# A two-layer hybrid decoder trunk on one core: statistics sent in 128-byte pieces, a held ScalarE half of a split, and 512-column projections

## The chip, the core and the metric

The kernel runs on one core of a Trainium2 chip. The core has a matrix engine (TensorE, PE in the profile; its weight loads are listed apart as PEld), a vector engine (VectorE, DVE), a scalar engine (ScalarE, ACT), GpSimd (POOL), and SyncE (SP), which here only issues transfers. Sixteen DMA engines move data between the large off-chip memory (HBM) and the on-chip memory (SBUF); matmuls write to PSUM, which has eight banks of 128 x 512 float32. Each engine takes its own instructions strictly in the order in which they stand in its queue, so one instruction that waits holds up all behind it.

The metric is device time in microseconds (us) of one execution. Lower is better.

## What is computed

256 tokens of width 1024 pass through two layers. Each layer does

```
h = layer_norm(a*x + 0.5*swiglu(x, ffn1))          # swiglu: (silu(x@Wg) * (x@Wu)) @ Wdown, Wdown 2816 x 1024
o = [deltanet(h), window_attention(h), memory_attention(h, mem_n)]
h = layer_norm(a*h + (sum_n sigmoid(gate_n) * (o_n @ w_branch_n)) @ w_out)
h = layer_norm(a*h + 0.5*swiglu(h, ffn2))
```

with a = (2*2)**0.25. `mem_n` is a layer norm of 256 memory rows, computed once: `(mem - mean) * rsqrt(var + 1e-5) * g + b`. All weights are float32 and each is used once, so the kernel reads some 220 MB of weights.

## The kernel before

**Three products for one.** Each weight tile arrives in float32 (`raw`, 128 x 1024, 512 KB) and is split in two: ScalarE rounds it to a shorter format (`whi`, line 116) and VectorE takes the remainder (`wlo`, line 117). Activations are split in the same way (`hT`, `u0` to `u10`, `w0` to `w3`). `mm3` then makes three matmuls: high x high, high x low, low x high. One raw tile with its two halves is a *unit*. There are three `raw` buffers and five each of `whi` and `wlo`; `unit` asks for a load on SyncE's queue and gives it a priority 300 places ahead of the program, so loads and splits run ahead of the matmuls as far as buffers allow.

**A feed-forward block (`Ffn`)** has eleven steps of 256 hidden columns. In a step four units make two banks (tokens 0 to 127 and 128 to 255; gate columns in the left half, up columns in the right). `out(i, banks)` then applies silu on ScalarE (line 339) and the product on VectorE (line 340), transposes 32 x 32 blocks on VectorE (line 343), and turns the rest through HBM: four small stores (`tr<-t`, line 349) and a load (`pt<-tr`, line 350), all on GpSimd's queue. `settle` splits the landed `pt` into the high and low halves of `u_i` (ScalarE's is the 128 x 512 cast `u<-pt`, VectorE's follows). The settlement of step i stands in `out(i+2)`, and those of the last two steps in the down projection. `issue_after(x)` adds, for the instructions inside it, an order behind `x` on the engine of `x` only. `settle` gives it a VectorE instruction in `out` and a matmul in the down projection, so ScalarE's cast was free to stand anywhere in ScalarE's queue that the scheduler chose.

**The down projection (`projA`)** takes 22 units of 128 x 1024 (the output projection of the mixers takes 8). The first two units (`lead`) are run for one half of the tokens and then for the other; the following ones for both in turn; the last 4 or 6 (`tail`) bank by bank, so that each bank is finished while the next is still computed. `full_rows` gives the banks: tokens 0 to 127 have two of 512 columns, tokens 128 to 255 have one of 512 (`c`), one of 256 (the left half of `d`) and one of 256 in another pool (`at`). The short last banks keep the work after the last matmul small. `Post` adds each finished bank to the residual (`src`, line 394) and does the layer norm.

**The memory statistics** are made beside the first layer's first feed-forward block: `mid` hangs pieces on certain steps. `rows_` computes mean and 1/std for 256 rows into `mst` (one number a partition, four columns), stores them to HBM transposed (line 454) and loads them back to all partitions as `gB` (line 456). `half(0)` and `half(1)` subtract, scale and split (lines 466 to 471), and `keep` stores the result (`mdr`, line 431, four transfers of 512 KB) for the second layer. Lines 454, 456, 349 and 350 share GpSimd's queue.

**Places in SBUF.** The pool `pu` hands out places in the order in which its tags are first asked for, each rounded up to 32 bytes of a partition: `hT`, `u0`, `u1`, `u2`, then `mst` (16 bytes, takes 32), `mgb` (64), `w0` to `w3`, `u3` and the rest. The pools `p2` and `p3` follow.

Of the kernel before, what the change touches and what calls it, by code (L numbers as in the profile page):

```python
# [17 lines left out]
P = 128  # L18
# [20 lines left out]
def tile_trunk(ctx, tc, x, xT, mem, memT_, wst, lnp, memln, cvw, rows, cst, out):  # L39
# [54 lines left out]
        nc.scalar.copy(t.rearrange("p v k -> p (v k)"), zero.to_broadcast([P, 2 * S]))  # L94


    pos = [0]

    def unit(w=U, dst=None, cuts=1, behind=None):
        ahead = tc.high_priority(offset=AHEAD) if pos[0] >= 8 * P * U else nullcontext()  # L100
        raw = T(praw, [P, U], "raw")
        src = wst[pos[0]:pos[0] + P * w].rearrange("(p w) -> p w", p=P)
        pos[0] += P * w
        (ph, th), (pl, tl) = dst or ((phi, "whi"), (plo, "wlo"))
        with ahead:
            hi = T(ph, [P, U], th, F32R)
            lo = T(pl, [P, U], tl, F32R)
            for i in range(cuts):
                c = slice(i * w // cuts, (i + 1) * w // cuts)
                nc.sync.dma_start(raw[:, c], src[:, c])  # L110
                with tc.issue_after(behind) if behind else nullcontext():
                    split(hi[:, c], lo[:, c], raw[:, c])
        return hi, lo

    def split(hi, lo, src):
        nc.scalar.copy(hi, src)  # L116
        return nc.vector.tensor_tensor(lo, src, hi.bitcast(F32), op=ALU.subtract).ins  # L117

    pinned = [False]

# [10 lines left out]
    def mm3(o, l, r, first, last, skip=False):  # L131
        (lh, ll), (rh, rl) = l, r
        matmul(o, lh, rh, start=first, stop=False, skip_group_check=skip)
        matmul(o, lh, rl, start=False, stop=False, skip_group_check=skip)
        return matmul(o, ll, rh, start=False, stop=last, skip_group_check=skip).ins

    def weave(work, steps):

# [31 lines left out]
            (b,) = yield from projB_parts(xt, 2, 4)  # L170
            use(i, b)

    def projA(xt, w, kpu, nk, outs, tail=0, dsts=(), lead=0, after=None, behind=None, held=(), led=None, along=None):

        def one(k, kk, hi, lo, tb, j):
            ts = slice(tb * P, (tb + 1) * P)
            n = [o.shape[-1] for o in outs[tb]]
            c = kk * w + sum(n[:j])
            c = slice(c, c + n[j])
            return mm3(outs[tb][j], (xt[0](k)[:, ts], xt[1](k)[:, ts]), (hi[:, c], lo[:, c]), k == 0, k == nk - 1)  # L180

        nu = nk // kpu
        units = {}

        def get(uu):
            if uu not in units:
                t = uu - (nu - tail)
                units[uu] = unit(kpu * w, dsts[t] if 0 <= t < len(dsts) else None, behind=behind if uu in held else None)
            return units[uu]

        def run(us, tb, js):
            ins = None
            for uu in us:
                for kk in range(kpu):
                    for j in js:
                        ins = one(uu * kpu + kk, kk, *get(uu), tb, j)
            return ins

        for tb in range(2):
            if lead:  # L200
                run(range(lead), tb, range(len(outs[tb])))
            if led:
                led(tb)
        for uu in range(lead, nu - tail):
            for tb in range(2):
                ins = run([uu], tb, range(len(outs[tb])))
# [88 lines left out]
    class Ffn:  # L295
# [37 lines left out]
        def out(self, i, banks):  # L333


            t = T(p2, [P, 8, 2, 32], "t2", bufs=4)
            for tb in range(2):
                g, u = (banks[tb][:, c:c + S].rearrange("p (j x) -> p j x", j=8) for c in (0, S))
                nc.scalar.activation(t[:, :, tb, :], g, AF.Silu)  # L339
                ins = nc.vector.tensor_tensor(t[:, :, tb, :], t[:, :, tb, :], u, op=ALU.mult).ins  # L340
            self.last = ins
            z = T(p2, [P, 512], "t2", bufs=4)
            ins = nc.vector.transpose(z, t.rearrange("p j t x -> p (j t x)")).ins  # L343
            if len(self.due) > 1:
                self.settle(ins)
            y = T(p2, [P, D], "pt")[:, 0:512]
            d = T(pd, [4, 32, 4, P], "tr")
            for q in range(4):
                nc.gpsimd.dma_start(d[:, :, q].rearrange("b c x -> c b x"), z[32 * q:32 * q + 32].rearrange("c (b x) -> c b x", b=4))  # L349
            nc.gpsimd.dma_start(y, d.rearrange("b c q x -> (b c) (q x)"))  # L350
            self.due.append((i, y))

        def settle(self, behind):

            if self.due:
                i, y = self.due.pop(0)
                hi, lo = (self.h(i)[:, n].rearrange("p a (t q s) -> p (a t) q s", t=2, q=4) for n in range(2))
                with tc.issue_after(behind):
                    split(hi, lo, y.rearrange("p (q n s) -> p n q s", q=4, n=4))

        def rest(self, hT, tail, dsts, post, mid={}, behind=None):
            for i in range(1, NFT // 2):
                banks = [acc() for _ in range(2)]
                for uu in range(KD // 2):
                    hi, lo = unit(behind=behind if i == 1 and uu < 2 else None)
                    for kk in range(2):
                        k, c = 2 * uu + kk, slice(kk * 512, kk * 512 + 512)
                        for tb in range(2):
                            ts = slice(tb * P, (tb + 1) * P)
                            mm3(banks[tb], (hT[0][:, k, ts], hT[1][:, k, ts]), (hi[:, c], lo[:, c]), k == 0, k == KD - 1)  # L370
                self.out(i, banks)
                for f in (2 * i, 2 * i + 1):
                    if f in mid:
                        with tc.issue_after(self.last):
                            mid[f]()
            outs = full_rows()
            projA((lambda k: self.hu[k // 2][:, 0, k % 2, :], lambda k: self.hu[k // 2][:, 1, k % 2, :]), D, 1, NFT, outs, tail, dsts, 2, post, along=self.settle)
# [41 lines left out]
    def memory_T(mT, l):  # L419
# [11 lines left out]
                nc.gpsimd.dma_start(mdr[i], flat(t.bitcast(F32)))  # L431

        def vecs():
            got["st"] = T(pu, [P, 2, 2], "mst")
            got["gb"] = T(pu, [P, 2, KD], "mgb")
            load(got["gb"], memln)
            mT.extend(T(pu, [P, 4, S], f"w{i}", F32R) for i in range(4))
            got["m"] = [T(p2, [P, D], "pp") for _ in range(2)]
            for tb in range(2):
                load(got["m"][tb], mem[tb * P:(tb + 1) * P, :])  # L440

        def rows_():
# [11 lines left out]
            nc.gpsimd.dma_start(d.rearrange("a t p -> p a t"), got["st"])  # L454
            got["row"] = T(pu, [P, D], "gB")[:, 0:512]
            nc.gpsimd.dma_start(got["row"], d.rearrange("a t p -> (a t p)").partition_broadcast(P))

        def halves_():
            got["m"] = [T(p2, [P, 4, S], "pp") for _ in range(2)]
# [27 lines left out]
    def mixers(l, hT, mkT, mv_, post):  # L487
# [519 lines left out]
        def between(tb):  # L1007
            if tb == 0:
# [1 line left out]
                    merge_turn(1, q)  # L1010
                pinned[0] = False

        outs = full_rows()
        projA((lambda k: mgT[k // 4][:, k % 4, :], lambda k: mgT[2 + k // 4][:, k % 4, :]), D, 1, KD, outs, 6,
              [((pu, a), (pu, b)) for a, b in (("u6", "u7"), ("u10", "u11"), ("u12", "u13"), ("u0", "u1"), ("u2", "u3"), ("u8", "u9"))], 2, post, led=between)


    hT = new_hT()
# [129 lines left out]
```

## Time and profile before

| | |
|---|---|
| median of three timed runs | 1311.1 us (1308.61 to 1311.26) |
| the profiled execution's own time | 1317.82 us |
| its span, first to last instruction | 1315.8 us |
| mean granted TensorE clock | 0.99 |
| busy: PE, DVE, ACT, POOL | 1279.6, 849.7, 658.9, 197.8 us |
| HBM read, written | 247.45 MB, 14.81 MB |

The profile is one execution. Its own time is 2.0 us more than its span, and 6.7 us more than the median of the timed runs. PE's busy time counts overlapping matmuls, so it is nearly the whole span even though a single stretch may contain waits; these are found in the rows for stretches and in the timeline.

In rows of a stretch (the view of windows) stand: the stretch in us from the span's start, its length, then busy time and number of instructions of PE, PEld, DVE, ACT and POOL, the granted TensorE clock (1.00 is full), the mean busy share of the DMA engines, and GB/s. In rows of the timeline: start, duration, engine, line, operation, tiles, count, and in brackets the idle time before it with what ended it. In rows of the chain: start, duration, what. In rows of the waits: who waited for whom, us in total, times, longest. In rows on DMA issues: the transfer, the queue, the count, KB each, median us from issue to landing.

### The profile page before, as it was taken

Reading aid. Unit: us, or ns where it says so; the run is one execution under the profiler, and the core shown is the slowest. Engines: PE = TensorE matmul, PEld = TensorE weight load, DVE = VectorE, ACT = ScalarE, POOL = GpSimd, SP = SyncE. Lnnn points to the kernel's source line nnn. Section 1 sums busy time; section 2 is a strip of 40 time slices with the busy share of each in tenths; the row PEclk is TensorE's granted clock in tenths of the full one; section 3 lists DMA queues with packets and bytes.
Section 4 is the critical chain, followed back from the end, with each engine's and each line's share of the span. In section 5 each row is a group of like instructions: output and inputs, shape, how many; then the busy total and the mean of one; then the engine's idle time right before and its main releaser. Section 6 shows DMA issues by size and latency. Waiting matters only on the chain.

```text
span 1315.8 us, 19159 instructions
## 1 busy us (share of the span) xinstructions
PE 1279.6 (97%) x7160; PEld 1091.7 (83%) x7160; DVE 849.7 (65%) x1266; ACT 658.9 (50%) x979; POOL 197.8 (15%) x357
## 2 busy tenths in 40 slices
PE   8997799999999999999999999999999999999997
PEld 6885688999878788888878888899988787888786
DVE  5575547598564875665576665658966378666655
ACT  5544444565674444553444544446566654444441
POOL 0221200101411002221012220001023100022100
PEclk9998899999999999999999999999999999999999
DMA  7887765664643557786767786656554356477662
GB/s 258 297 266 182 241 221 169 193 189 147 160 145 114 181 170 226 240 254 214 251 205 252 241 259 212 207 162 208 167 145 156 97 175 225 145 253 250 224 207 105
DMA packets 77980, 263.52 MB, mean 200 GB/s; under 512 B 11872, under 2 KB 13024, under 8 KB 77888
## 3 DMA queue, kind: packets, MB, share of 16 engines
q1 hardware_dynamic: 66320, 232.53, 55.4%
q0 software_dynamic: 11568, 29.77, 7.6%
q8 instruction: 56, 0.92, 0.3%
q14 instruction: 36, 0.29, 0.1%
HBM read 247.45 MB, written 14.81 MB: 199 GB/s over the span
## 4 chain that ended last, share of the span: by engine, by line
PE 73%; DMA 13%; DVE 5%; ACT 5%; issue 3%; POOL 1%; SPq 0%; DVEq 0%; ACTq 0%; POOLq 0%
PE acc L126 62%; DMA raw<-in_wst_dram 8%; PE at L126 4%; DMA pt<-tr 3%; ACT whi L116 3%; PE sm L126 3%; DVE wlo L117 2%; DMA tr<-t 2%; PE sm L129 1%; DMA ms<-mst 1%; PE acc L321 1%; PE acc L318 1%; PE acc L319 1%; PE at L129 0%; POOL tr L349 0%
## 5 line engine op out<-in xcount | busy, mean ns | idle before, releaser
L117 DVE TENSOR_TENSOR wlo<-raw,whi 128x1024 fp32r<-128x1024 f32 (+2 forms) x403 | 483.3, 1212 | 352.4 <-ACT whi L116 350.9
L116 ACT CAST whi<-raw 128x1024 fp32r<-128x1024 f32 (+2 forms) x403 | 412.1, 1035 | 391.7 <-DMA raw<-in_wst_dram 222.2
L126 PE MATMUL acc<-whi,hT 128*128 128x512 f32 (+1 forms) x1824 | 567.7, 389 | 10.6 <-ACT whi L116 10.6
L126 PEld LDWEIGHTS acc<-whi,hT 128*128 128x128 f32 x1824 | 343.2, 190 | 80.4 <-ACT whi L116 11.8
L126 PE MATMUL acc<-wlo,hT 128*128 128x512 f32 (+1 forms) x912 | 353.3, 387 | 2.0 <-DVE wlo L117 1.9
L126 PE MATMUL acc<-whi,u 128*128 128x512 f32 (+1 forms) x800 | 253.0, 380 | 9.2 <-DVE t L340 9.2
L126 PEld LDWEIGHTS acc<-wlo,hT 128*128 128x128 f32 x912 | 172.9, 190 | 36.9 <-DVE wlo L117 4.3
L126 PEld LDWEIGHTS acc<-whi,u 128*128 128x128 f32 x800 | 152.4, 191 | 40.2 <-DVE t L340 9.3
L349 POOL DMA_DIRECT2D tr<-t x176 | 96.2, 553 | 387.9 <-DVE t L343 374.8
L126 PE MATMUL acc<-wlo,u 128*128 128x512 f32 (+1 forms) x400 | 150.6, 376 | 0.4 <-DVE wlo L117 0.4
L126 PE MATMUL acc<-hT,whi 128*128 128x256 f32 x672 | 122.2, 284 | 0.0
L126 PEld LDWEIGHTS acc<-hT,whi 128*128 128x128 f32 x672 | 104.7, 192 | 0.0
L126 PE MATMUL acc<-hT,wlo 128*128 128x256 f32 x336 | 95.1, 283 | 0.0
L126 PEld LDWEIGHTS acc<-wlo,u 128*128 128x128 f32 x400 | 76.8, 192 | 14.7 <-DVE wlo L117 0.8
L116 ACT CAST u<-pt 128x512 fp32r<-128x512 f32 x44 | 27.3, 620 | 105.5 <-DMA pt<-tr 105.5
L126 PEld LDWEIGHTS acc<-hT,wlo 128*128 128x128 f32 x336 | 64.4, 192 | 0.0
L350 POOL DMA_DIRECT2D pt<-tr x44 | 24.6, 558 | 156.3 <-DMA tr<-t 83.4
L117 DVE TENSOR_TENSOR u<-pt,u 128x512 fp32r<-128x512 f32 x44 | 29.0, 660 | 22.7 <-ACT u L116 22.7
L126 PE MATMUL at<-whi,u 128*128 128x256 f32 x152 | 39.7, 287 | 0.0
L340 DVE TENSOR_TENSOR t<-t,acc 128x256 f32<-128x256 f32 x88 | 36.3, 416 | 4.6 <-ACT t L339 3.5
L339 ACT ACTIVATE t<-acc 128x256 f32<-128x256 f32 x88 | 32.6, 376 | 10.6 <-PE acc L126 10.3
L516 DVE SCALAR_TENSOR_TENSOR t<-acc,cw,t 128x255 f32<-128x255 f32 (+2 forms) x72 | 34.5, 479 | 0.9
(249 smaller groups left out, 1263.5 us busy)
## 6 DMA issues: line engine op xcount, KB each, us to landing
raw<-in_wst_dram SPq DMA_DIRECT2D x409, 512.0 KB, 4.4
tr<-t POOLq DMA_DIRECT2D x176, 64.0 KB, 3.2
pt<-tr POOLq DMA_DIRECT2D x44, 256.0 KB, 4.9
raw<-in_wst_dram SPq DMA_DIRECT2D x16, 324.0 KB, 3.1
gB<-in_lnp_dram SPq DMA_DIRECT2D x6, 512.0 KB, 6.5
bB<-in_lnp_dram SPq DMA_DIRECT2D x6, 512.0 KB, 5.9
mdr<-w POOLq DMA_DIRECT2D x4, 512.0 KB, 7.2
w<-dr POOLq DMA_DIRECT2D x4, 512.0 KB, 12.2
```

The source lines that it names most:

```text
L116: nc.scalar.copy(hi, src)
L117: return nc.vector.tensor_tensor(lo, src, hi.bitcast(F32), op=ALU.subtract).ins
L126: return pe(nc.tensor.matmul(*a, **k))
L129: return pe(nc.tensor.transpose(*a))
L318: nc.tensor.matmul(ps, hT[0][:, k, ts], hi[:, c], start=k == 0, stop=False)
L319: nc.tensor.matmul(ps, hT[0][:, k, ts], lo[:, c], start=False, stop=False)
L321: nc.tensor.matmul(ps, hT[1][:, k, ts], hi[:, c], start=False, stop=k == KD - 1)
L339: nc.scalar.activation(t[:, :, tb, :], g, AF.Silu)
L340: ins = nc.vector.tensor_tensor(t[:, :, tb, :], t[:, :, tb, :], u, op=ALU.mult).ins
L349: nc.gpsimd.dma_start(d[:, :, q].rearrange("b c x -> c b x"), z[32 * q:32 * q + 32].rearrange("c (b x) -> c b x", b=4))
L350: nc.gpsimd.dma_start(y, d.rearrange("b c q x -> (b c) (q x)"))
L516: nc.vector.scalar_tensor_tensor(yc[:, j, d:], b[:, j, :S - d], w[:, t:t + 1], yc[:, j, d:], op0=ALU.mult, op1=ALU.add)
```

## The change

It has three parts.

1. **Statistics.** `mst` becomes 128 x 2 x 32 floats (256 bytes of a partition), cleared by GpSimd; mean and 1/std of both row halves stand in the first four columns of its first plane. VectorE transposes that plane in 32 x 32 blocks into the second, and four stores of 4 partitions x 128 bytes take the place of the one store of 512 single numbers. The load of `gB` stays.
2. **Held splits.** `settle` holds ScalarE's cast behind the second silu of its step too, besides VectorE's half behind the block transpose. In the down projection the two last settlements stand after units 2 and 10 (before: 2 and 5), held behind the last unit's own split on both engines (before: behind a matmul, which holds neither).
3. **Columns.** Tokens 128 to 255 have two banks of 512 columns up to the tail. Then `early` adds bank `d` to the residual, and only the tail's units go to two fresh banks of 256 columns. Per unit before the tail that is 12 matmuls of 512 columns where there were 9 of 512 and 6 of 256.

```diff
-    pos = [0]
+    pos, newest = [0], []
...
                 with tc.issue_after(behind) if behind else nullcontext():
-                    split(hi[:, c], lo[:, c], raw[:, c])
+                    newest[:] = split(hi[:, c], lo[:, c], raw[:, c])
...
     def split(hi, lo, src):
-        nc.scalar.copy(hi, src)
-        return nc.vector.tensor_tensor(lo, src, hi.bitcast(F32), op=ALU.subtract).ins
+        return nc.scalar.copy(hi, src).ins, nc.vector.tensor_tensor(lo, src, hi.bitcast(F32), op=ALU.subtract).ins
...
+            first = k == ((nu - tail) * kpu if tb and j and ends and len(outs[1]) > 2 else 0)
...
-            return mm3(outs[tb][j], (xt[0](k)[:, ts], xt[1](k)[:, ts]), (hi[:, c], lo[:, c]), k == 0, k == nk - 1)
+            mm3(outs[tb][j], (xt[0](k)[:, ts], xt[1](k)[:, ts]), (hi[:, c], lo[:, c]), first, k == nk - 1 or bool(ends and tb and j and k == (nu - tail) * kpu - 1))
...
-            if along and uu in (2, 5):
-                along(ins)
+            if along and uu in (2, 10):
+                along(*newest)
         for uu in range(nu - tail, nu):
             get(uu)
         turns = ()
+        if ends:
+            after.early(outs[1].pop())
+            outs[1] += ends
...
-        return [[a, b], [c, d[:, 0:S], at()[:, 0:S]]]
+        return [[a, b], [c, d]], [at()[:, 0:S] for _ in range(2)]
...
-                nc.scalar.activation(t[:, :, tb, :], g, AF.Silu)
+                act = nc.scalar.activation(t[:, :, tb, :], g, AF.Silu).ins
...
-                self.settle(ins)
+                self.settle(act, ins)
...
-        def settle(self, behind):
+        def settle(self, act, vec):
...
-                with tc.issue_after(behind):
+                with tc.issue_after(act), tc.issue_after(vec):
...
+        def early(self, bank):
+
+            y = hres[1][:, 512:]
+            nc.vector.scalar_tensor_tensor(y, bank, 0.5 / ALPHA, y, op0=ALU.mult, op1=ALU.add)
...
-            got["st"] = T(pu, [P, 2, 2], "mst")
+            got["st"] = T(pu, [P, 2, 32], "mst")
+            nc.gpsimd.memset(got["st"], 0.0)
...
-                rsqrt(got["st"][:, 1, tb:tb + 1], mv[:, 1:2], T(p3, [P, 1], "rst"))
-            d = T(pd, [2, 2, P], "ms")
-            nc.gpsimd.dma_start(d.rearrange("a t p -> p a t"), got["st"])
+                rsqrt(got["st"][:, 0, 2 + tb:3 + tb], mv[:, 1:2], T(p3, [P, 1], "rst"))
+            d = T(pd, [4, P], "ms")
+            nc.vector.transpose(got["st"][:, 1], got["st"][:, 0])
+            for q in range(4):
+                nc.gpsimd.dma_start(d[:, 32 * q:32 * q + 32], got["st"][32 * q:32 * q + 4, 1])
```

The callers pass the new `ends` on; nothing else is touched.

More of the change, by code (lines that the diff above doesn't have):

```diff
@@ L134, in mm3 @@
         matmul(o, lh, rl, start=False, stop=False, skip_group_check=skip)
-        return matmul(o, ll, rh, start=False, stop=last, skip_group_check=skip).ins
+        matmul(o, ll, rh, start=False, stop=last, skip_group_check=skip)
     def weave(work, steps):
@@ L171, in halves, with projA @@
             use(i, b)
-    def projA(xt, w, kpu, nk, outs, tail=0, dsts=(), lead=0, after=None, behind=None, held=(), led=None, along=None):
+    def projA(xt, w, kpu, nk, outs, tail=0, dsts=(), lead=0, after=None, behind=None, held=(), led=None, along=None, ends=()):
         def one(k, kk, hi, lo, tb, j):
@@ L191, in run @@
         def run(us, tb, js):
-            ins = None
             for uu in us:
@@ L195, in run @@
                     for j in js:
-                        ins = one(uu * kpu + kk, kk, *get(uu), tb, j)
-            return ins
+                        one(uu * kpu + kk, kk, *get(uu), tb, j)
         for tb in range(2):
-            if lead:
-                run(range(lead), tb, range(len(outs[tb])))
+            run(range(lead), tb, range(len(outs[tb])))
             if led:
@@ L205, in projA @@
             for tb in range(2):
-                ins = run([uu], tb, range(len(outs[tb])))
-            if along and uu in (2, 5):
-                along(ins)
+                run([uu], tb, range(len(outs[tb])))
+            if along and uu in (2, 10):
+                along(*newest)
         for uu in range(nu - tail, nu):
```

10 lines of the change are left out of this document (5 added, 5 removed).

## The prediction

> **What bounds the kernel now.** I read the page first, then two equal stretches by the view of windows, then the waits and the timeline around the slow one. From the page, the chain:
>
> ```profile
> PE 73%; DMA 13%; DVE 5%; ACT 5%; issue 3%; POOL 1%; SPq 0%; DVEq 0%; ACTq 0%; POOLq 0%
> ```
>
> The chain that sets the end is PE for three quarters; an edit pays where PE waits or where its clock is cut, and hardly anywhere else. The waits of PE, and below them the wait that part 2 of the change aims at:
>
> ```profile
> PE acc L126 <- ACT whi L116: 10.6, 3, 5.3
> PE acc L126 <- DVE t L340: 9.2, 5, 4.3
> ```
>
> ```profile
> ACT u L116 <- DMA pt<-tr: 105.5, 37, 7.1
> ```
>
> So PE's two large waits come to 19.8 us in the whole program; most of ScalarE's 105.5 us do not reach PE. Where PE's waits lie is seen by comparing the same work in both layers: from the first silu of step 6 of the first feed-forward block to the first line 394 (88.9 to 205.8 us in layer 0, 746.3 to 845.1 in layer 1).
>
> ```profile
> 88.90:205.80 116.90, 103.08 (x461) 83.49 (x460) 67.00 (x97) 51.08 (x65) 17.84 (x32) 0.91 0.76 231
> 746.30:845.10 98.80, 98.80 (x484) 83.27 (x483) 56.58 (x61) 46.16 (x54) 13.64 (x25) 1.00 0.74 240
> ```
>
> The same matmuls take 116.9 us in layer 0 and 98.8 in layer 1, where PE is never idle and the clock full. The difference, 18.1 us, is all that can be had there: 13.8 of it is idle PE (116.9 - 103.1), the rest a clock of 0.91. Inside it:
>
> ```profile
> 100.00:105.00 5.00, 4.34 (x20) 3.25 (x18) 0.00 (x1) 0.29 (x1) 0.00 (x0) 1.00 0.68 34
> ...
> 145.00:150.00 5.00, 1.02 (x5) 0.49 (x3) 2.33 (x3) 1.33 (x2) 1.79 (x4) 0.83 1.00 406
> ```
>
> At 100 to 105 us the DMA engines are 68% busy and move only 34 GB/s: they chew tiny pieces. GpSimd's timeline and the DMA issues name them:
>
> ```profile
> 95.94 0.77 POOL L454 DMA_DIRECT2D ms<-mst  x1 [6.15 <-DVE mst L256]
> 96.70 1.65 POOL L349 DMA_DIRECT2D tr<-t  x3
> 107.42 0.56 POOL L456 DMA_DIRECT2D gB<-ms  x1 [9.08 <-DMA ms<-mst]
> 107.97 0.55 POOL L349 DMA_DIRECT2D tr<-t  x1
> 114.12 0.56 POOL L350 DMA_DIRECT2D pt<-tr  x1 [5.59 <-DMA tr<-t]
> ```
>
> ```profile
> tr<-t POOLq DMA_DIRECT2D x176, 64.0 KB, 3.2
> gB<-ms POOLq DMA_DIRECT2D x1, 256.0 KB, 5.8
> ms<-mst POOLq DMA_DIRECT2D x1, 2.0 KB, 11.2
> ```
>
> The store of 2 KB lands after 11.2 us, 32 times fewer bytes than `tr` in 3.5 times its time. It hurts twice. Weight loads issued beside it come late, and GpSimd's queue stands 9.08 us at `gB`, so the fourth `tr` leaves at 107.97 and `pt` at 114.12; ScalarE, in order, waits for both:
>
> ```profile
> 104.71 1.04 ACT L116 CAST whi<-raw 128x1024 fp32r<-128x1024 f32 x1 [5.96 <-DMA raw<-in_wst_dram]
> ...
> 117.39 0.62 ACT L116 CAST u<-pt 128x512 fp32r<-128x512 f32 x1 [6.01 <-DMA pt<-tr]
> ```
>
> The second dip (from 145) has another cause: `keep` writes there, the engines are 100% busy at 406 GB/s, and splits run late behind the first dip.
>
> **Part 1, the statistics.** Removed: one store of 512 pieces. Added: four stores of 4 pieces, each 0.55 us to issue (1.65 / 3 for `tr`), 2.2 us in all against 0.77. The last leaves near 95.94 + 2.2 = 98.1. No row has a store of 128-byte pieces; from above I bound its landing by the 5.5 us of the fourth `tr` (it ends the 5.59 us wait before `pt`), from below by 0, and take `tr`'s median 3.2. So `gB` can leave at about 101.3 instead of 107.42 and land by its 5.8 at 107.1 (109 at the upper bound) instead of 113.26. The added block transpose is a sixteenth of line 343's, under 0.2 us of VectorE; the clearing is early and small on GpSimd. A wait is moved, not removed: VectorE stands at line 466 until `gB` is there, and behind it are the `wlo` that feed PE.
>
> ```profile
> 113.28 1.23 DVE L466 TENSOR_TENSOR pp<-pp,gB 128x1024 f32<-128x1024 f32 x1 [0.61 <-DMA gB<-ms]
> ```
>
> If VectorE comes to line 466 earlier by the 9.08 us that the queue stood, near 104, it waits there some 3 us (5 with `gB` at 109). I leave 3 us of stall for that and 2 us for the second dip, where `keep`'s 2 MB must still be written: 18.1 - 5 = 13.1 us gained. Bounds: 18.1 if layer 0 runs as layer 1, and 6 (107.42 - 101.3) if only the waiting at the store goes and the dips otherwise repeat.
>
> The page "DMA: Bandwidth & Descriptors" of the Trainium skill (Specifications) speaks against this size: below 512 bytes a transfer still pays a read-modify-write, and 128 bytes is below. By it the piece costs what a 4-byte piece costs; an estimate from the row above, 11.2 us over 32 pieces for each of 16 engines, is 0.35 us a piece, so at most 1.4 us for four in a row, and the sum would not move by more.
>
> **Part 2, the held casts.** ScalarE now meets `u<-pt` two steps after its transfer, so the 105.5 us of waiting mostly go; their worth is only where a late `whi` reaches PE. Outside the stretch above that is one place:
>
> ```profile
> 1238.62 0.62 ACT L116 CAST u<-pt 128x512 fp32r<-128x512 f32 x1 [3.55 <-DMA pt<-tr]
> 1239.14 2.95 ACT L116 CAST whi<-raw 128x1024 fp32r<-128x1024 f32 x3
> ...
> 1245.21 1.04 ACT L116 CAST whi<-raw 128x1024 fp32r<-128x1024 f32 x1 [2.86 <-DMA raw<-in_wst_dram]
> ```
>
> ```profile
> 1247.90 0.58 PE L126 MATMUL acc<-whi,u 128*128 128x256 f32 x1 [2.60 <-DVE t L340]
> ```
>
> ```profile
> 1245.00:1250.00 5.00, 2.40 (x10) 2.00 (x9) 2.74 (x4) 2.36 (x4) 0.00 (x0) 0.74 0.88 287
> ```
>
> The cast waits 3.55 us for `pt`; three raw buffers stay full behind it, the next load starts late, its `whi` waits 2.86 us, the second silu (in the queue right behind it) comes late, and PE waits 2.60 us for the bank. The clock then falls (0.74 over 5 us, 1.3 us lost). With the cast behind the silu the three `whi` run at once. Worth 3.9 at most; I take 3. What takes its place: `pt` has two buffers and is freed by VectorE's half, which was held already, so no transfer starts later; 0.62 us of ScalarE moves, none is added.
>
> The page "TensorE: Matmul & The Clock Gate" of the Trainium skill (Part 1, the HAM clock gate) says that the array falls to half speed after an idle window of about 3.4 us. By it the 2.60 us wait would cost no clock, and neither would my leftover 3 and 2 us. Here the trace does not agree: 2.60 us idle, and a clock of 0.74 follows. By the page the sum would be some 1.3 us better.
>
> **Part 3, the columns.** One 512-column matmul takes the place of two of 256, 3 x 2 x (18 + 16) pairs in the four down projections and 12 in the two output projections: 216 pairs.
>
> ```profile
> 179.46 0.28 PE L126 MATMUL acc<-wlo,u 128*128 128x256 f32 x1
> 179.58 0.28 PE L126 MATMUL acc<-whi,u 128*128 128x256 f32 x1
> ...
> 180.05 0.39 PE L126 MATMUL acc<-whi,u 128*128 128x512 f32 x1
> 180.29 0.40 PE L126 MATMUL acc<-wlo,u 128*128 128x512 f32 x1
> ```
>
> ```profile
> 434.17 0.39 PE L126 MATMUL acc<-wlo,hT 128*128 128x512 f32 x1
> 434.40 0.62 PE L126 MATMUL acc<-whi,hT 128*128 128x512 f32 x2
> 434.85 0.39 PE L126 MATMUL acc<-wlo,hT 128*128 128x512 f32 x1
> ```
>
> Durations mislead here, since matmuls overlap; the steps from start to start count. 0.12 us for 256 columns, 0.24 for 512: two halves cost a whole, and the count of instructions is free. Beside `hT` a 512-column step is 0.227 us ((434.85 - 434.17) / 3). A unit of twelve then costs 2.72 to 2.82 us against the 2.82 of before (its rows stand with the rivals), so 0 to 0.10 us for 72 units: 0 to 7 us. I take 1.5, near the row with `u`. `early` adds six of line 394's additions on VectorE beside the tail, hidden by matmuls; uncovered they would cost 0.7 us each. The work after the last matmul is the same.
>
> **Sum.** 13.1 + 3 + 1.5 = 17.6 us. The profiled execution would go from 1317.8 to 1300.2 us; the timed runs lie 6.7 us below the profiled one, and if the stalls are as long in them, 1311.1 - 17.6 = **1293.5 us**.
>
> **Rivals.**
> *Moved tiles.* The wider `mst` moves `w0` to `w3`, `u3` and all behind them by 224 bytes. A down projection's period changes when its stationary operand passes from `u1`, `u2` to `u3` and on:
>
> ```profile
> 166.16 2.42 PE acc L126 x12
> 168.58 0.36 PE at L126 x3
> 168.94 2.46 PE acc L126 x12
> ```
>
> These are units 5 and 6, the last with `u2` and the first with `u3`: 2.42 + 0.36 = 2.78 us, then 2.82. `hT`, `u0` to `u2` and `whi` all lie 32 bytes past a multiple of 512; `u3` and `w0` lie at 128 past one, and go to 352. If the step of 0.235 (2.82 / 12) instead of 0.227 comes from that, and 352 cures it, some 1030 matmuls of 512 columns (counted from the loops: down and output projections, branches, memory values) gain 8 ns each: 8 us more, 1285.5. For it: the switch stands exactly at `mst`. Against: nothing shows that 352 counts like 32.
> *Half.* The dips are those of full DMA engines (406 GB/s at 145 to 150), and only the wait at the store goes: 6 + 1 = 7 us, 1304.
> *No effect.* The scheduler leaves the casts, and `gB` arrives late anyway: 1311.
> *In series (slower).* GpSimd lets the four stores run one after the other, each landing before the next: 4 x 5.5 = 22 us to `gB` instead of 11.2. VectorE then stands some 11 us longer at line 466: 1311.1 + 11 - 4.5 = 1317.6. It decides once the four take over 16 us. Against: the three `tr` leave 0.55 us apart.
>
> **How the numbers follow.** Forecast 0.6, moved tiles 0.17, half 0.15, no effect 0.04, in series 0.04. A measurement tells about 0.2% (2.6 us) from no change. Faster by more 0.92, within 0.04, slower 0.04. The range reaches from 1311.1 - 18.1 - 3.9 - 1.5 - 8 = 1279.6, about 1280, to half's 1304, with its bound of 6 alone 1305.
>
> **What would show it.** Right: no stretch near 34 GB/s at 68% busy; `gB` leaves within 6 us of the statistics; the layer 0 stretch falls to 100 to 106 us; `u<-pt` waits under 20 us in all; no idle PE near 1245. Moved tiles: 512-column steps of 0.227 us beside `u3` and on. Wrong: a new VectorE wait at line 466 of over 5 us, or PE idle near 145 as now.

## The result, and the profile after

| | before | after |
|---|---|---|
| median of the timed runs | 1310.68 us (1308.61 to 1311.26, 4 runs) | 1293.11 us (1289.72 to 1294.92, 4 runs) |
| the profiled execution's own time | 1317.82 us | 1294.92 us |
| its span | 1315.8 us | 1293.1 us |
| mean granted TensorE clock | 0.990 | 0.995 |

The ratio is 0.9866, with a 95% interval of 0.9842 to 0.989: 17.6 us less (14.4 to 20.7). The two profiled executions differ by 22.9 us, because the one of before is the slowest of its kernel (that of the changed kernel is the slowest of its four, too); sizes below are therefore taken from ratios (times 1311 us), and the profiles say where the time lies. The lines of `after` are shifted: the matmuls are line 125, both halves of a split line 116, the first use of `gB` line 474 (466 before).

The chain that ended last, and two lines of the waits (who waited for whom, us in total, times, longest):

```profile
PE 83%; DMA 7%; DVE 4%; ACT 3%; issue 2%; POOL 0%; SPq 0%; DVEq 0%; ACTq 0%; POOLq 0%
```

```profile
PE acc L125 <- DVE t L340: 5.9, 4, 3.4
PE acc L125 <- ACT whi L116: 5.0, 1, 5.0
```

```profile
ACT u L116 <- DMA pt<-tr: 14.4, 5, 4.8
```

PE's share of the chain rose from 73 to 83%. Its two large waits fell from 19.8 to 10.9 us; 5.3 and 5.0 of these are the first load of the program. ScalarE's waits for `pt` fell from 105.5 to 14.4 us. Now the stretches of the same work in layer 0, first silu of step 6 to the first line 399 (394 before), and three pieces of it:

```profile
85.30:193.29 107.99, 101.62 (x421) 81.18 (x420) 67.44 (x99) 51.98 (x66) 19.29 (x35) 0.95 0.74 252
100.00:105.00 5.00, 5.00 (x24) 4.14 (x23) 1.88 (x3) 2.94 (x5) 0.57 (x1) 1.00 0.79 266
130.00:135.00 5.00, 4.05 (x12) 2.90 (x12) 4.96 (x7) 2.77 (x4) 2.75 (x5) 0.75 0.95 326
135.00:140.00 5.00, 1.55 (x5) 0.50 (x3) 2.14 (x4) 1.83 (x3) 0.18 (x1) 0.84 0.90 347
```

The 34 GB/s at 100 to 105 us have become 266, and PE is busy there. What is left is a second dip at 125 to 146 us. GpSimd's queue and the DMA issues show the new statistics:

```profile
92.66 0.56 POOL L349 DMA_DIRECT2D tr<-t  x1 [2.81 <-DVE mst L460]
93.20 2.06 POOL L462 DMA_DIRECT2D ms<-mst  x4
95.25 1.68 POOL L349 DMA_DIRECT2D tr<-t  x3
99.35 0.57 POOL L464 DMA_DIRECT2D gB<-ms  x1 [2.42 <-DMA tr<-t]
```

```profile
gB<-ms POOLq DMA_DIRECT2D x1, 256.0 KB, 5.3
ms<-mst POOLq DMA_DIRECT2D x4, 0.5 KB, 3.6
```

Four stores issue in 2.06 us and land after 3.6 us (median; 2.8 to 4.1, against 11.2 before), and `gB` waits 2.42 us instead of 9.08. The profile puts the end of that wait down to a landing of `tr`, whose three stores were issued behind the four. Where the time went, by stages: from the first matmul of a stage in the trace to the first of the next, in us. The first two rows are the first feed-forward block of layer 0. Each column is one execution, so a row shows where time lies, not what a part is worth.

| stage | before | after |
|---|---|---|
| gate and up, layer 0, block 1 | 136.9 | 125.4 |
| down projection, layer 0, block 1 | 71.6 | 70.4 |
| gate and up of the other three blocks | 121.2, 121.4, 121.0 | 121.1, 121.3, 120.9 |
| down projection of the other three | 63.9, 61.7, 65.7 | 61.5, 61.1, 60.9 |
| the two output projections | 26.0, 25.4 | 24.8, 25.4 |

The three undisturbed blocks run at 121 and 61 us. The first block of layer 0 still stands about 13 us above them.

### The profile page after: what moved, and what is told of

The parts are those of the page before. It is cut to its first block, busy times and chain, and to the rows that moved or that the text cites. A ratio compares the mean times of both kernels' runs of the same rounds, so it can differ in the third digit from the quotient of the medians.

```text
span 1293.1 us, 18743 instructions
## 1 busy us (share of the span) xinstructions
PE 1269.7 (98%) x6944; PEld 1076.4 (83%) x6944; DVE 855.6 (66%) x1273; ACT 662.0 (51%) x979; POOL 201.2 (16%) x361
## 4 chain that ended last, share of the span: by engine, by line
PE 83%; DMA 7%; DVE 4%; ACT 3%; issue 2%; POOL 0%; SPq 0%; DVEq 0%; ACTq 0%; POOLq 0%
PE acc L125 72%; DMA raw<-in_wst_dram 6%; PE at L125 4%; PE sm L125 3%; DVE wlo L116 2%; ACT whi L116 2%; PE sm L128 1%; PE acc L321 1%; PE acc L318 1%; PE acc L319 1%; PE at L128 1%; DVE u L116 0%; DMA gB<-ms 0%; DMA tr<-t 0%; ACT pp L724 0%
## 5 line engine op out<-in xcount | busy, mean ns | idle before, releaser
L125 PE MATMUL acc<-whi,u 128*128 128x512 f32 x784 | 256.1, 400 | 5.9 <-DVE t L340 5.9
L125 PEld LDWEIGHTS acc<-whi,u 128*128 128x128 f32 x784 | 149.2, 190 | 42.2 <-DVE t L340 4.8
L125 PE MATMUL acc<-wlo,u 128*128 128x512 f32 x392 | 155.8, 398 | 0.0
L116 ACT CAST u<-pt 128x512 fp32r<-128x512 f32 x44 | 27.0, 613 | 14.4 <-DMA pt<-tr 14.4
L125 PE MATMUL acc<-whi,w 128*128 128x512 f32 x96 | 31.7, 401 | 2.1 <-DVE w L116 2.1
## 6 DMA issues: line engine op xcount, KB each, us to landing
w<-dr POOLq DMA_DIRECT2D x4, 512.0 KB, 10.6
```

The source lines that it names most:

```text
L116: return nc.scalar.copy(hi, src).ins, nc.vector.tensor_tensor(lo, src, hi.bitcast(F32), op=ALU.subtract).ins
L125: return pe(nc.tensor.matmul(*a, **k))
```

## The experiments

Each is one kernel; its ratio is to the kernel before on the same chip. Two things are read from each trace beside the time: the idle stretches of PE, and the **lead**, by which the end of a unit's `wlo` on VectorE precedes the unit's first matmul. As long as the lead is positive PE does not wait for a cast; a small lead means that the next delay reaches PE.

### Which part is worth what

**p1_statistics_only.** Before, with part 1 alone.

```diff
...
-            nc.gpsimd.dma_start(d.rearrange("a t p -> p a t"), got["st"])
...
+            nc.vector.transpose(got["st"][:, 1], got["st"][:, 0])
+            for q in range(4):
+                nc.gpsimd.dma_start(d[:, 32 * q:32 * q + 32], got["st"][32 * q:32 * q + 4, 1])
```

> Part 1 alone on the kernel before. My theory: the tiny pieces of the one store cause the first dip of layer 0 by themselves, so the feed-forward block of layer 0 (first matmul to 142.2 us before) loses its waits between 104 and 121 us and ends some 9 to 12 us earlier; the wait near 1245 us stays; total 1298 to 1302 us. Rival: the casts that wait for pt leave PE too little lead, so without part 2 a wait of over 3 us stays between 100 and 125 us and the gain is under 7 us (over 1304).

1304.51 us (6 runs), ratio 0.9942 (0.9915 to 0.9968): 7.6 us (4.2 to 11.1). That is a miss of my theory in size. The time is over the rival's 1304, but the wait that the rival asks for is not in this trace (its row stands below).

**p2_held_casts_only.** Before, with part 2 alone.

```diff
-                self.settle(ins)
+                self.settle(act, ins)
...
-                with tc.issue_after(behind):
+                with tc.issue_after(act), tc.issue_after(vec):
```

> Part 2 alone. My theory: the wait of 2.60 us near 1245 us and the lowered clock behind it go, u<-pt waits under 20 us in all, the layer 0 dips stay; 3 to 5 us gained, 1306 to 1308 us. Rival: the casts only matter beside the late transfers of layer 0, or the held casts also keep layer 0 ahead of the store: then under 2 us, or over 8.

1303.44 us (4 runs), ratio 0.993 (0.9904 to 0.9957): 9.2 us (5.6 to 12.6), three times the predicted 3. The rival's threshold of over 8 us was met, though the interval reaches below it.

**p3_columns_only.** Before, with part 3 alone.

```diff
...
-        return [[a, b], [c, d[:, 0:S], at()[:, 0:S]]]
+        return [[a, b], [c, d]], [at()[:, 0:S] for _ in range(2)]
...
```

> Part 3 alone, mst narrow as before, so u3 and all behind it stay where they were. My theory: units beside u0 to u2 cost 2.72 us instead of 2.78, those beside u3 and on 2.80 to 2.81 instead of 2.82; 0.3 to 0.7 us for each projection, 1.5 to 3 us in all, 1308 to 1310 us. Rival: the shift of the tiles by 224 bytes made the 2.80 us of the changed kernel; then 2.81 to 2.82 here beside u3 and on, and under 1 us in all.

1310.78 us (10 runs), ratio 0.9999 (0.9975 to 1.0022): nothing that can be told from no change, nor from the expected 1.5 to 3 us (the interval ends at 3.3).

**parts_1_and_3 and parts_2_and_3.** The changed kernel with one part undone.

```diff
...
-                with tc.issue_after(act), tc.issue_after(vec):
+                with tc.issue_after(behind):
```

> The changed kernel without part 2 (casts free to stand anywhere, settlements after units 2 and 5 behind a matmul). If parts 1 and 2 each take away their own waits, the loss is what part 2 won alone, 8 us (1301 us). Rival, both cure the same dip of layer 0: the loss is under 5 us (under 1298 us), most of it the wait in the last feed-forward block.

```diff
...
-            for q in range(4):
-                nc.gpsimd.dma_start(d[:, 32 * q:32 * q + 32], got["st"][32 * q:32 * q + 4, 1])
...
+            nc.gpsimd.dma_start(d.rearrange("a t p -> p a t"), got["st"])
```

> The changed kernel without part 1 (one store of 512 single numbers; mst narrow, so u3 and all behind it at the old place). If the parts add up, the loss is what part 1 won alone, 7 us (1300 us), with waits of PE of some 3 us in all between 100 and 115 us and a landing of ms near 11 us. Rival: with part 2's lead of four units the store is covered; the loss is under 4 us.

Without part 2: 1304.45 us (6 runs), ratio 0.9955 (0.9935 to 0.9976), 5.9 us. Without part 1: 1301.52 us (4 runs), ratio 0.9923 (0.9902 to 0.9945), 10.1 us. So part 2, added last, is worth 17.6 - 5.9 = 11.7 us, and part 1 17.6 - 10.1 = 7.5. Alone they gave 9.2 and 7.6. Within the intervals, which are some 3 us each way and wider for a difference of two, parts 1 and 2 add up; the rivals by which each makes the other needless (a loss under 5 us without part 2, under 4 without part 1) get no support. Part 2 comes out larger both ways, but the intervals do not part the two.

What part 2 changes in layer 0 is seen in ScalarE's timeline 40 us ahead of the first dip (start, duration, engine, line, operation, tiles, count, idle before). First without part 2, then the changed kernel:

```profile
56.53 0.38 ACT L341 ACTIVATE t<-acc 128x256 f32<-128x256 f32 x1
61.82 0.62 ACT L116 CAST u<-pt 128x512 fp32r<-128x512 f32 x1 [4.91 <-DMA pt<-tr]
62.34 2.94 ACT L116 CAST whi<-raw 128x1024 fp32r<-128x1024 f32 x3
```

```profile
57.85 0.38 ACT L339 ACTIVATE t<-acc 128x256 f32<-128x256 f32 x1
58.13 0.61 ACT L116 CAST u<-pt 128x512 fp32r<-128x512 f32 x1
58.90 1.05 ACT L116 CAST whi<-raw 128x1024 fp32r<-128x1024 f32 x1 [0.16 <-DMA raw<-in_wst_dram]
```

Without part 2 the cast waits 4.91 us, and three `whi` pile up behind it. No matmul is late, so no wait of PE shows it, but the lead falls from 4.04 us at unit 20 to 0.01 at unit 21. In the changed kernel it goes from 3.33 to 3.26. In before it falls to 0.17, and at units 29 to 34, ahead of the statistics' disturbance, it is 0.7 to 1.5 us, against 3.7 to 4.3 after. The held casts thus keep the cushion on which the memory work then falls. In the execution without part 2 PE is idle again near 110 us, right behind another late cast (ScalarE's and PE's timeline):

```profile
108.78 0.62 ACT L116 CAST u<-pt 128x512 fp32r<-128x512 f32 x1 [6.43 <-DMA pt<-tr]
```

```profile
110.39 0.50 PE L125 MATMUL acc<-whi,hT 128*128 128x512 f32 x1 [2.00 <-ACT whi L116]
111.65 0.50 PE L125 MATMUL acc<-wlo,hT 128*128 128x512 f32 x1 [0.76 <-DVE wlo L116]
```

What the lost lead costs is not shown, however. The profiled execution of part 1 alone, the fastest of its six (1299.71 us), has a lead as small (0.42 us at unit 21, -0.1 to 0.5 at units 37 to 43), and PE is all but never idle at the first dip, at full clock:

```profile
96.00:125.00 29.00, 28.80 (x127) 23.26 (x126) 22.11 (x24) 17.19 (x25) 9.41 (x18) 1.00 0.83 257
```

So the store of single numbers is one source of the first dip; that the early casts are the other is seen in the execution above and argued from the leads. At the end of the program the stall near 1245 is gone with part 2, as predicted: the last down projection takes 61.5 us with part 2 alone, and 63.2 to 65.8 us in the four profiles without part 2.

### The moved tiles

**tiles_32_past_512.** The changed kernel with 192 bytes more for `mst`, so that `w0` to `w3`, `u3` and all behind them stand 32 bytes past a multiple of 512, as `hT`, `u0` to `u2` and `whi` do.

```diff
-            got["st"] = T(pu, [P, 2, 32], "mst")
+            got["st"] = T(pu, [P, 112], "mst")[:, 0:64].rearrange("p (a n) -> p a n", a=2)
```

> The changed kernel with mst wider by 192 bytes more, so that w0 to w3, u3 and all behind lie 32 bytes past a multiple of 512, as hT, u0 to u2, whi and wlo do. If the places of the two operands relative to each other set the step: 512-column matmuls of whi and wlo beside u3 and on step by 0.227 us instead of 0.233, a unit of twelve costs 2.72 us everywhere, 5 to 8 us gained (1285 to 1288 us). Rival: the step hangs on something else that changes at u3 (which tiles, how far apart they are); then 2.80 us stays and the time is that of the changed kernel, 1293 us.

The same part of the down projection, PE's timeline, first of the changed kernel and then of this one (a row of two matmuls has no row for the second):

```profile
164.68 0.39 PE L125 MATMUL acc<-wlo,u 128*128 128x512 f32 x1
164.91 0.63 PE L125 MATMUL acc<-whi,u 128*128 128x512 f32 x2
...
167.48 0.39 PE L125 MATMUL acc<-wlo,u 128*128 128x512 f32 x1
```

```profile
168.71 0.39 PE L125 MATMUL acc<-wlo,u 128*128 128x512 f32 x1
168.94 0.61 PE L125 MATMUL acc<-whi,u 128*128 128x512 f32 x2
...
171.43 0.39 PE L125 MATMUL acc<-wlo,u 128*128 128x512 f32 x1
```

Twelve steps take 2.80 us in the one and 2.72 in the other: 0.233 and 0.227 us a matmul. The place in SBUF alone sets this. Yet the time is 1292.25 us (4 runs), ratio 0.9845 (0.9817 to 0.9872), 1 to 3 us better than the changed kernel and not told apart from it: the down projections of the three undisturbed blocks go from 61.5, 61.1, 60.9 to 60.5, 60.1, 59.9, and the expected 5 to 8 us do not appear in the time. The second output projection even took 27.75 us in that execution.

### The second dip

In the changed kernel VectorE waits for `gB` as the prediction said, 3 us at 104:

```profile
104.68 1.23 DVE L474 TENSOR_TENSOR pp<-pp,gB 128x1024 f32<-128x1024 f32 x1 [3.04 <-DMA gB<-ms]
```

Behind this wait the lead goes from 4.75 us (unit 36) to 1.14 (unit 37), stays near 1 and is -0.80 at unit 43; then PE waits at 125 to 141 us:

```profile
130.42 0.47 PE L125 MATMUL acc<-whi,u 128*128 128x512 f32 x1 [1.68 <-DVE t L340]
...
140.24 0.79 PE L125 MATMUL acc<-whi,u 128*128 128x512 f32 x1 [3.44 <-DVE t L340]
```

Both waits are for a bank (the product at line 340 frees it), not for a cast. ScalarE's timeline shows what stands ahead of the last four silus of gate and up:

```profile
127.45 1.04 ACT L116 CAST w<-pp 128x1024 fp32r<-128x1024 f32 x1
128.40 0.64 ACT L339 ACTIVATE t<-acc 128x256 f32<-128x256 f32 x2
...
133.13 1.04 ACT L116 CAST whi<-raw 128x1024 fp32r<-128x1024 f32 x1 [1.69 <-DMA raw<-in_wst_dram]
134.08 0.38 ACT L339 ACTIVATE t<-acc 128x256 f32<-128x256 f32 x1
137.55 1.04 ACT L116 CAST whi<-raw 128x1024 fp32r<-128x1024 f32 x1 [3.09 <-DMA raw<-in_wst_dram]
138.50 0.38 ACT L339 ACTIVATE t<-acc 128x256 f32<-128x256 f32 x1
```

The two silus at 128.40, ahead of the wait of 1.68 us, come right behind the halves' work (`w<-pp`). The last one, ahead of the wait of 3.44 us, stands behind a cast that waits 3.09 us for its load when the halves' work on ScalarE is over, while the DMA engines are 90 to 95% busy (the rows at 130 and 135).

Suspects were `keep`'s stores, the wait for `gB`, and the halves' own work. Two runs did not do what their edit meant:

**stores_after_memory_kv.** `keep` called behind `memory_kv`.

```diff
+        keep = mid.pop(19, None)
...
         kv = memory_kv(mT, post.end)
+        if keep:
+            keep()
```

> The changed kernel with the four stores of the normalised memory (2 MB) moved from the first feed-forward block to behind the memory projections. My theory: the dip left at 125 to 146 us comes of these stores, which slow the weight loads to 6 to 7 us; then PE's waits there fall under 3 us and the time to 1286 to 1288 us. Rival: the lead is lost before, at VectorE's wait for gB (3.04 us) and in the memory work on VectorE and ScalarE; then the dip stays over 5 us and the time over 1290 us.

**memory_in_down.** `half(0)`, `half(1)` and `keep` called behind units 4, 7 and 11 of the down projection.

```diff
+            if 100 + uu in hooks:
+                hooks[100 + uu]()
...
-        ... 15: lambda: half(0), 17: lambda: half(1), 19: keep}
+        ... 104: lambda: half(0), 107: lambda: half(1), 111: keep}
```

> The changed kernel with both halves of the memory's normalisation and their stores hung on units 4, 7 and 11 of the first down projection, where no transposes and few transfers run. By either theory of the dip the gate and up part of layer 0 then takes 121 to 123 us as in the other three blocks; the down part 61 to 64 us if the work is hidden there; 1284 to 1287 us in all. Against it: the down part keeps a wait of over 4 us, since VectorE has 3.7 us more of work for each half there.

They gave 1295.75 us (ratio 0.9882, 0.9863 to 0.9902) and 1292.74 (0.9862, 0.984 to 0.9883), with the dip. But the traces show that nothing had moved: the scheduler may place what is not held, and it put the stores of the first and the halves of the second where they had been (GpSimd's timeline of the first, VectorE's of the second):

```profile
114.21 0.56 POOL L436 DMA_DIRECT2D mdr<-w  x1 [0.54 <-ACT w L116]
...
129.16 0.54 POOL L436 DMA_DIRECT2D mdr<-w  x1 [0.89 <-DVE w L116]
```

```profile
103.30 1.23 DVE L476 TENSOR_TENSOR pp<-pp,gB 128x1024 f32<-128x1024 f32 x1 [5.11 <-DMA gB<-ms]
```

Both are second measurements of the changed kernel and decide nothing about the stores. The following kernels hold the halves by `issue_after`.

**half_one_step_later.**

```diff
-        ... 15: lambda: half(0), 17: lambda: half(1), 19: keep}
+        ... 16: lambda: half(0), 18: lambda: half(1), 20: keep}
```

> The changed kernel with half(0), half(1) and keep one step of FFN 1 later (16, 18 and 20 instead of 15, 17 and 19), so that VectorE reaches the product that reads gB about 5.8 us later, when gB has landed (104.65 us in the changed kernel's profile). My theory, that the second dip is the rest of TensorE's lead over the casts lost where VectorE waits 3.04 us for gB and then has the halves' work ahead of the casts: no wait for gB at the first of these products, the lead of the casts stays over 1.5 us through unit 40, and the dip behind 125 us is at least halved; gate and up of this block 119 to 123 us instead of 125.4 and the time 1284 to 1290 us. Rival, the halves' own work (about 8.6 us of VectorE at 1.23 us a product or cast, beside the casts of the units) is enough without any wait: the lead falls below 1 us all the same, 5.8 us later, the gate and up take 124 to 126 us and the time stays at 1291 to 1296 us.

1293.06 us (4 runs), ratio 0.9839 (0.9815 to 0.9862). The wait for `gB` is gone (the first product, at 111.39, has no idle time before it):

```profile
111.06 0.41 DVE L340 TENSOR_TENSOR t<-t,acc 128x256 f32<-128x256 f32 x1
111.39 1.22 DVE L474 TENSOR_TENSOR pp<-pp,gB 128x1024 f32<-128x1024 f32 x1
```

The lead stays at 4.8 to 6.5 us from unit 35 to 43, gate and up take 122.7 us, and yet the down projection takes 68.3 and PE has one long wait:

```profile
136.14 0.77 PE L125 MATMUL acc<-whi,u 128*128 128x512 f32 x1 [4.08 <-DVE t L340]
```

So neither theory was right as I put it: the lead was kept, and the dip moved and stayed. A lost lead is thus not what makes the second dip, and neither is the wait for `gB` alone. PE waits here not for a cast but for a bank. ScalarE's timeline shows why:

```profile
129.31 1.05 ACT L116 CAST whi<-raw 128x1024 fp32r<-128x1024 f32 x1 [3.51 <-DMA raw<-in_wst_dram]
130.26 2.07 ACT L478 ACTIVATE pp<-pp,mgb 128x256 f32<-128x256 f32 x4
132.24 1.03 ACT L116 CAST whi<-raw 128x1024 fp32r<-128x1024 f32 x1
133.18 1.04 ACT L116 CAST w<-pp 128x1024 fp32r<-128x1024 f32 x1
134.12 0.64 ACT L339 ACTIVATE t<-acc 128x256 f32<-128x256 f32 x2
```

The last two silus, whose banks the down projection needs, were ready when gate and up ended at 127.59. They run at 134.12: ahead of them in the queue stand a cast that waits 3.51 us for its load (which landed after 6.45 us, beside two of `keep`'s stores), four activations of `half(1)` (2.07 us) and two more casts.

**halves_held_in_down.** As memory_in_down, with the pieces really held:

```diff
+            if 100 + uu in hooks:
+                with tc.issue_after(newest[0]), tc.issue_after(newest[1]):
+                    hooks[100 + uu]()
```

> The changed kernel with half(0), half(1) and keep taken out of the gate and up of FFN 1 and held behind the casts of units 4, 7 and 11 of its down projection. My theory, that the second dip comes of the halves' work and wait ahead of the casts in the gate and up: gate and up of this block take 120 to 122 us as the other three blocks do (121.1 to 121.4), with no idle TensorE from 96 to 140 us; the down projection, whose units take about 1 us longer on TensorE than they need on VectorE, gives back 0 to 5 us; time 1283 to 1289 us. Rival, the dip belongs to the place where the down projection begins, whatever ran before (the units' loads, or the last steps' transposes): the gaps behind 125 us stay over 5 us in sum, gate and up stay at 124 us or more, or the down projection takes over 75 us; time 1291 us or more.

1290.05 us (4 runs, 1285.35 to 1291.06), ratio 0.9815 (0.979 to 0.9841): 6.7 us below the changed kernel by the ratios. The windows of the two dips, and the last silus on ScalarE:

```profile
96.00:125.00 29.00, 29.00 (x129) 24.01 (x129) 20.08 (x25) 15.43 (x21) 9.61 (x18) 1.00 0.88 276
125.00:146.00 21.00, 21.00 (x95) 17.34 (x94) 16.17 (x17) 12.37 (x18) 3.88 (x7) 1.00 0.74 221
```

```profile
127.77 0.39 ACT L342 ACTIVATE t<-acc 128x256 f32<-128x256 f32 x1 [0.98 <-PE acc L125]
128.45 1.05 ACT L116 CAST whi<-raw 128x1024 fp32r<-128x1024 f32 x1 [0.29 <-PE acc L125]
129.40 0.38 ACT L342 ACTIVATE t<-acc 128x256 f32<-128x256 f32 x1
```

PE is never idle from 96 to 146 us, the clock is full, the last silus run when their banks are done or one cast later, and the down projection takes 61.1 us like the others. Gate and up took 122.95 us, a little over the expected 122. The rival, that the dip belongs to the beginning of the down projection whatever runs before, falls. By the ratio the time is 1286.7 us of 1311, inside the expected 1283 to 1289; the median itself, on a chip where before took 1313.21, is not. Two things limit the reading. The profile is the fastest of the four executions, and no trace shows what the other three (1289.81 to 1291.06 us) lost. And `keep`'s stores, which need the halves, moved with them: they are issued at 144.8 to 150.0 us, against 113.9 to 130.2 in the changed kernel.

**later_and_stores_held.** half_one_step_later, with `keep` placed in the down projection inside the same hold.

```diff
-        ... 20: keep}
+        ... 111: keep}
```

> The kernel of half_one_step_later with keep's four stores of 512 KB held behind the casts of unit 11 of the down projection, so that they leave after 140 us instead of at 120 to 136 us. In half_one_step_later the wait for gB is gone and a dip remains (one gap of 4.1 us at 131.7 to 136.1, half clock after it); the loads issued beside the stores land after 6.45 and 6.74 us, others after 3.6 to 5.5 us. Theory A, these stores lengthen the loads and that alone makes the remaining dip: no PE gap over 0.6 us from 96 to 145 us, ScalarE's waits for raw below 8 us in 96 to 150 us, down projection of this block 61 to 63 us instead of 68.3, time 1284 to 1289 us. Theory B, ScalarE's and VectorE's work for the halves, queued ahead of the last steps' bank-freeing products and casts, is enough without the stores: the gap of over 3 us stays between 125 and 140 us, the down projection takes 66 us or more, time 1290 to 1295 us.

1292.28 us (4 runs, 1286.71 to 1293.27), ratio 0.9847 (0.9825 to 0.9869). The hold is on ScalarE and VectorE, and the stores are on GpSimd's queue, so it did not hold them:

```profile
119.07 0.56 POOL L439 DMA_DIRECT2D mdr<-w  x1 [0.60 <-ACT w L116]
...
133.89 0.54 POOL L439 DMA_DIRECT2D mdr<-w  x1 [0.90 <-DVE w L116]
```

It is thus a second measurement of half_one_step_later, and a useful one: with the stores in the same place PE waits only 1.58 us, not 4.08, and the profiled execution, with a down projection of 62.9 us, is 1286.71 us:

```profile
134.07 0.47 PE L125 MATMUL acc<-whi,u 128*128 128x512 f32 x1 [1.58 <-DVE t L343]
```

The size of this dip differs between executions of nearly the same order of work. What the stores by themselves add was not tried and stays open.

**held_in_down_and_tiles.** halves_held_in_down with the wider `mst` of tiles_32_past_512 (the two diffs above).

> The kernel of halves_held_in_down with mst 192 bytes wider, so that the later tiles stand 448 bytes from where they stood before the change and the products with u3 and later go at 2.72 us a unit (tiles_32_past_512) instead of 2.80. The two gains should add up: four down projections whose units with u3 to u15 get 0.08 us a unit faster, some 1 us a block, and output projections unchanged: 1284 to 1288 us and a ratio to before of 0.978 to 0.982. If the clock or the loads set the end of the down projection, nothing is gained over halves_held_in_down (ratio 0.9815).

1283.79 us (5 runs, 1281.65 to 1290.87), ratio 0.9786 (0.9759 to 0.9812): the fastest kernel of this study, 10.5 us below the changed one by the ratios and 28.1 below before. The down projections take 61.0, 60.5, 60.1 and 59.9 us. Whether the tiles add to the held halves cannot be told (0.9786 against 0.9815, the intervals overlap); that the whole is faster than the changed kernel can. Against tiles_32_past_512 it differs in the hold alone, and there the intervals lie apart (0.9845 with 0.9817 to 0.9872, and 0.9786 with 0.9759 to 0.9812): moving the halves and their stores is worth 7.7 us.

## Why the prediction was right in the sum, and where not in its terms

**The sum** was 17.6 us and the measurement 17.6 (14.4 to 20.7). The terms were 13.1, 3 and 1.5; the runs give 7.5, 9 to 12, and nothing that can be measured. Both misses are larger than the intervals (4.2 to 11.1 for part 1 alone, 5.6 to 12.6 for part 2 alone). Two errors of size cancelled, so that the total agrees to 0.1 us is luck.

**Part 1 (13.1, measured 7.5).** The mechanism held: the stretch of 34 GB/s is gone, a piece lands after 3.6 us (3.2 taken), GpSimd's wait before `gB` is 2.42 us, and the wait of VectorE that takes its place is 3.04 us where 3 were left for it. `gB` was issued 6.7 us behind the statistics (92.66 to 99.35), just over the 6 given. The step that failed is "2 us for the second dip". It is 11.8 us in the profiles, if halves_held_in_down is the block without it: (125.4 + 70.4) - (122.95 + 61.07). These are the slowest execution of the one kernel and the fastest of the other; by the ratios the two kernels are 6.7 us apart, which is still three times the 2. The stretch accordingly fell from 116.9 to 108.0, not to 100 to 106. I had put the second dip down to full DMA engines and to lateness inherited from the first. With the first dip gone, the second stayed. It comes of the memory work beside the last steps of gate and up: it goes when the halves and `keep`'s stores are moved together (halves_held_in_down, held_in_down_and_tiles), and stays when only the wait for `gB` is taken away (half_one_step_later). How much of it is the halves' own work and how much the stores, beside which loads come late, is open. The 1.4 us that the prediction allowed for the small pieces cannot be told from the 0.4 us by which they land later than `tr`'s median. The prediction's sign that would make it wrong, PE idle near 145 as before, was there, 10 us earlier.

**Part 2 (3, measured 9 to 12).** The stall near 1245 went as worked out: all four waits of PE for line 340 in the changed kernel (5.9 us) lie at 130 to 141, and the last down projection went from 65.7 to 60.9 us in the profiles. What failed is "outside the stretch above that is one place". The worth inside the stretch was left out, since all of its 18.1 us had been given to part 1; yet the prediction's own row with `u<-pt` at 117.39, 6.01 us late, lies there. And a wait that does not reach PE was priced at nothing, although it takes lead that a later delay may need; how many us that lead is worth in layer 0 is argued, not shown.

The page "TensorE: Matmul & The Clock Gate" of the Trainium skill (Part 1, the HAM clock gate) gives about 3.4 us of idling before half speed, in a window that runs freely. In the changed kernel a wait of 1.68 us and one of 0.53 are followed by a granted clock of 0.75 (130 to 135 us), so by the trace shorter waits already cost clock; of a free-running window these runs can show neither the length nor the phase. By the page's rule the stall near 1245 would have cost 2.60 us and not 3.9, so the sum would have been 1.3 us smaller; the prediction's "1.3 us better" has the wrong sign.

**Part 3 (1.5, measured 0.1, -2.9 to 3.3).** Not to be told. The profiles show units of the first three tiles going from 2.78 to 2.72 us and later ones from 2.82 to 2.80, some 2 us in all, which agrees with the value taken.

**The rivals.** *Moved tiles*: the cause was right and the cure wrong. At 352 bytes past a multiple of 512 the step is 0.233 us, not 0.227; at 32 it is. *Half* had part 1 nearly right (6, measured 7.5), but the wait at the store was not all that went, since the first dip is gone; as a whole (1304) it is what the changed kernel gives without part 2. *In series* falls: the four stores issue in 2.06 us, and `gB` leaves 6.2 us behind the first of them. *No effect* falls.

## What to carry to other kernels

Look at what a wait that does not reach the bounding engine takes from the lead of the work queued behind it: here 4.91 us of ScalarE at 57 us cost nothing there and took the lead from 4.04 to 0.01 us; in that execution TensorE waited at 110 us, in another with as small a lead it did not. After an edit that moves work, find the moved instruction in the trace first, since an order that is not held, or held on another engine's queue, may leave it where it was. Where several edits touch one stretch, undo each of them from the whole as well as trying each alone; a right sum says nothing of its terms.

## What the runs showed of the hardware that was not expected

- A 512-column matmul step takes 0.227 or 0.233 us by the place of its operands in SBUF alone: the same program with the tiles 192 bytes further on went from 2.80 to 2.72 us a unit. Why 352 past a multiple of 512 differs from 32 was not tried further.
- A store of 2 KB as 512 single numbers takes 11.2 us and holds up its neighbours (the three `tr` behind it landed after 10.6 to 11.0 us, where their median is 3.2); the same numbers as 16 pieces of 128 bytes take 3.6 us.
- The clock: 1.68 and 0.53 us of waiting within 3.2 us were followed by a clock of 0.75. In later_and_stores_held a wait of 1.58 us cost none (1.00 in this row of its windows):

```profile
125.00:146.00 21.00, 19.41 (x87) 15.74 (x86) 11.78 (x13) 9.44 (x14) 5.76 (x11) 1.00 0.77 237
```
